# Turning the convolution branch, the heads' outputs and the memory's tokens with VectorE and transfers of GpSimd

## The chip, the cores and the metric

The kernel runs on one core of one Trainium2 chip. The core has five engines with instruction queues of their own: TensorE (PE, matrix products and transposes into PSUM), VectorE (DVE), ScalarE (ACT), GpSimd (POOL) and SyncE (SP, which here only issues transfers). Each queue runs in order; engines and transfers wait for one another through semaphores. The metric is the device time of one execution in microseconds (us), lower is better.

## The reference

One layer of a streaming encoder on 512 tokens x 1024 channels in float32, with 256 memory tokens. Cut to what the change touches:

```python
h = _rms_norm(x, norm_mix_pre)
(a_q, a_k, a_v, f_q, f_k, f_v, f_g, c_u, s_x, s_b, s_c) = jnp.split(h @ w_in, cuts, axis=-1)
# A: differential attention, 4 heads of 128 output channels, each normed per token over its channels
ya = _diff_attention(a_q, a_k, a_v, lam, t_pos)
ya = _rms_norm(ya, diff_norm) * (1.0 - lambda_init)
# B: forgetting attention, 8 heads of 64
yf = _forgetting_attention(f_q, f_k, f_v, log_f, t_pos)
# C: gated unit, causal depthwise convolution over 31 tokens, LayerNorm over 512 channels, swish
yc = _dwconv_causal(c_a * jax.nn.sigmoid(c_g), conv_dw) + conv_dw_b
yc = jax.nn.silu(_layer_norm(yc, conv_ln_g, conv_ln_b))
# D: short convolution;  then  sum over branches of sigmoid(gate) * (branch @ w_branch), @ w_out, norm, residual
# cross-attention: m = _rms_norm(mem, norm_mem); keys and values are m @ w_xkv
# gated MLP with a depthwise convolution over 3 tokens
```

The three places share one problem: a result lies with channels on the partitions and is to be normed over channels (so tokens must be on the partitions), or the reverse.

## The kernel before

Every float32 product is made of three passes: both operands are split into a high part (float32r) and the rest, and `mm3` issues high x high, high x low and low x high. ScalarE writes the high part of a weight block (L190), VectorE the rest (L191), ahead of TensorE. A block is [128 x 8 x 128] weights against 512 tokens: 24 matmuls of 512 columns. `run_blocks` takes the blocks in a fixed order (`mixer_jobs`): the convolution's inputs, the D branch, the gates of D, the values of A (`v_jobs`), queries and keys of the four A heads (`qk_jobs`) with the gates of C between them, the values of the forgetting branch (`vf_jobs`), its queries and keys for four pairs of heads with the gates of A between them, then the gates of the forgetting branch, the output projection, cross-attention and the MLP.

Everything else is a background task, a Python generator that the planner `Background` advances between blocks: the first two tasks of its queue, by a credit of 0.7 per microsecond of its own clock, each step giving its cost and the time that must pass before the next (`yield cost, wait`). `drain` runs a task out at once. Afterwards the framework orders the instructions of each engine; `issue_after` holds an instruction behind another one of the same engine.

The tasks that the change touches:

- `conv_norm_task` (L670): when the four convolutions have ended (their ends are in `conv_ends`), VectorE transposes the result in 32x32 blocks (L676), SP writes it to DRAM with 128-byte runs in four transfers (L680) and reads it back with tokens on the partitions in four more (L683); VectorE norms it (L693 to L696), and the same way leads back to channels (`conv_chan`). ScalarE then makes two passes for each of four tiles (L705, L706), which are split into y["c"].
- `a_task` (L822): six steps of scores, softmax and values of one A head, then the tail: ScalarE copies the output from PSUM (L858), TensorE transposes it in four pieces (L863), ScalarE squares (L864), VectorE sums (L866) and scales it (L868), TensorE transposes back (L874), and `split` with the scale `half["dn"]` writes y["a"] (L877).
- `mem_task` (L1169): for each of two tiles of 128 memory tokens, load, norm (`normed`), and `to_channels` (L286), which transposes in eight pieces on TensorE and splits into `ns.mt`.
- `f_task` (L965): loads two rows of cumulative sums (`ck`, L972), then per step GpSimd makes a bias (`fbias`, L1002, L1004), TensorE the scores, and VectorE adds the two and takes the maximum (L1008).

TensorE's own transposes all go through `transpose` (L236). The tags `ck` and `fbias` have two buffers of [128 x 512] each, as have PSUM's `mm`, `av`, `sc` and `tr`.

Of the kernel before, what the change touches and what calls it, by code (L numbers as in the profile page):

```python
# [25 lines left out]
P = 128  # L26
# [57 lines left out]
def hybrid_layer(ctx: ExitStack, tc: tile.TileContext, a: dict, out: bass.AP):  # L84
# [584 lines left out]

    def conv_norm_task():  # L670
        xn = m1p.tile([P, 5, S], F32, tag="qk", name="xn", bufs=2)
        tok, chan = (dram.tile([S, S], F32, name=n) for n in ("conv_tok", "conv_chan"))

        def turn(rows, squares, src):
            for i in range(4):
                V.transpose(squares[:, i], src[:, i])  # L676
                yield 0.65, 0.0
            form = rows.rearrange("(b r) (j a c) -> a r j b c", r=32, a=4, c=32)
            for a in range(4):
                SP.dma_start(form[a], squares[a * 32:a * 32 + 32].rearrange("r j (b c) -> r j b c", c=32))  # L680
            yield 0.0, 4.0
            for i in range(4):
                SP.dma_start(xn[:, i], rows[i * P:(i + 1) * P, :])  # L683
            yield 0.0, 5.0

# [3 lines left out]
        yield from turn(tok, conv_u, conv_y)  # L689
        for t in range(NT):  # L690
            st = m1p.tile([P, 6], F32, tag="bn6", name="bn6", bufs=2)
            mv = m1p.tile([P, 2], F32, tag="bn2", name="bn2", bufs=2)
            V.bn_stats(st, xn[:, t])  # L693
            V.bn_aggr(mv, st)
            r = rstd_of(m1p, [mv[:, 1:2]])
            V.tensor_scalar(xn[:, t], xn[:, t], mv[:, 0:1], r, ALU.subtract, ALU.mult)  # L696
            yield 1.5, 0.0
        yield from turn(chan, conv_y, xn)
# [4 lines left out]
        for j in range(4):  # L703
            e = e4()
            A.activation(e[:, 0], xn[:, j], AF.Identity, bias=pc("ln_b", j), scale=pc("ln_g", j))  # L705
            A.activation(e[:, 1], xn[:, j], AF.Tanh, bias=half["ln_b"][:, j:j + 1], scale=half["ln_g"][:, j:j + 1])  # L706
# [55 lines left out]

    def qk_jobs(cq, ck, j, then):
# [5 lines left out]
        def body_q(hi, lo):  # L769
# [5 lines left out]
            for c, r in enumerate(rows):  # L775
                A.copy(qk[r, c], ps[r])
                V.tensor_tensor(qk[rows[1 - c], c], ps[r], qk[r, c].bitcast(F32), ALU.subtract)  # L777
# [43 lines left out]

    def a_task(h, qk, v):  # L822
        es, pt, av = {}, None, None
        for step in range(6):
# [31 lines left out]
            if step == 5:  # L856
                e = e4()
                A.copy(e[:, 0], av)  # L858
            yield cost, 3.5

        ps = bank("tr")
        for t in range(NT):
            transpose(ps[:, t * P:(t + 1) * P], e[:, 0, t * P:(t + 1) * P])  # L863
        A.activation(e[:, 1], ps, AF.Square, scale=1.0 / math.sqrt(P))  # L864
        ms = m1p.tile([P, NT], F32, tag="ms4", name="ms4", bufs=2)
        V.tensor_reduce(ms, e[:, 1].rearrange("p (t c) -> p t c", t=NT), AX.X, ALU.add)  # L866
# [6 lines left out]
        for t in range(NT):  # L873
            transpose(ps2[:, t * P:(t + 1) * P], e[:, 0, t * P:(t + 1) * P])  # L874
# [880 lines left out]
```

## Time and profile before

| | |
|---|---|
| median of 3 runs | 1061.36 us (1061.24 to 1062.24) |
| profiled execution | 1061.46 us, span 1059.7 us |
| TensorE busy | 1048.7 us (99%) |
| VectorE, ScalarE, GpSimd busy | 800.8, 497.9, 150.8 us |
| transfers that GpSimd issues (queue q0) | 2560 packets, 8.54 MB |
| transfers that SP issues (queue q1) | 170659 packets, 124.10 MB |

In the profile's rows, "L232" is the line of the kernel, `out<-in` the tiles by the program's names, `128x512` partitions x elements. In an answer by line the three numbers are the shortest, middle and longest duration in ns, then the first and last start in us. In a timeline the first two columns are start and length in us, and brackets hold the idle time of the engine before the instruction and what ended it. In the list of waits come the waiting instruction, the one waited for, the total in us, the count and the longest.

### The profile page before, as it was taken

The page shows a single profiled execution, that of the slowest core. Times are in us where ns is not written, and L with a number is a line of the kernel's source. Part 1 is how long each engine was busy: PE and PEld are TensorE (multiplying, and loading weights), DVE is VectorE, ACT ScalarE, POOL GpSimd, SP SyncE. Part 2 cuts the span into 40 slices and gives each one's busy share as a digit, 9 for nine tenths or more (in the row PEclk, how much of TensorE's full clock was granted, in tenths as well). Part 3 has the DMA queues.
Part 4 walks back from the last instruction along what each step waited for, and adds up shares of the span by engine and source line. Part 5 has one row for each costly group of instructions (what it writes and reads, how often), then busy time and mean ns, then how long its engine had stood idle before and what let it go on. Part 6 is the DMA issues. An engine that isn't in the chain of part 4 may idle for free.

```text
span 1059.7 us, 14546 instructions
## 1 busy us (share of the span) xinstructions
PE 1048.7 (99%) x5343; PEld 891.8 (84%) x5343; DVE 800.8 (76%) x1270; ACT 497.9 (47%) x819; POOL 150.8 (14%) x249
## 2 busy tenths in 40 slices
PE   9999999999999999999999999999999999999997
PEld 8888888878888988888888899999888888888886
DVE  6999997577666358766575888886778788777796
ACT  5322222277465255655443665654333333445672
POOL 4001000100001015322100031031111211111011
PEclk9999999999999999999999999999999999999999
DMA  8854335732222243322344734226566776725662
GB/s 269 300 153 104 104 97 128 198 113 80 80 80 68 59 135 100 97 84 80 120 140 154 268 133 120 80 81 199 179 229 211 235 230 209 236 80 179 210 216 80
DMA packets 179773, 156.78 MB, mean 148 GB/s; under 512 B 22207, under 2 KB 151852, under 8 KB 179701
## 3 DMA queue, kind: packets, MB, share of 16 engines
q1 hardware_dynamic: 170659, 124.10, 38.9%
q10 hardware_dynamic: 6482, 23.21, 5.8%
q0 software_dynamic: 2560, 8.54, 2.8%
q8 instruction: 42, 0.69, 0.3%
q14 instruction: 30, 0.25, 0.1%
HBM read 135.89 MB, written 19.94 MB: 147 GB/s over the span
## 4 chain that ended last, share of the span: by engine, by line
PE 95%; DMA 1%; DVE 1%; ACT 1%; issue 0%; POOL 0%; SPq 0%; POOLq 0%; DVEq 0%; ACTq 0%
PE ps_mm L232 51%; PE ps_av L232 29%; PE ps_sc L232 7%; PE ps_tr L232 4%; PE ps_tr L236 3%; DMA xn<-conv_tok 1%; PE ps_mm L442 1%; PE ps_av L442 1%; DMA conv_chan<-y 0%; PE ps_mm L384 0%; SPq L680 0%; PE ps_sc L389 0%; DMA xn<-conv_chan 0%; DVE wl L191 0%; POOL st_r L271 0%
## 5 line engine op out<-in xcount | busy, mean ns | idle before, releaser
L190 ACT CAST wh<-wr 128x1024 fp32r<-128x1024 f32 (+1 forms) x142 | 148.6, 1049 | 273.5 <-PE ps_mm L232 185.6
L191 DVE TENSOR_TENSOR wl<-wr,wh 128x1024 fp32r<-128x1024 f32 (+1 forms) x142 | 178.1, 1256 | 80.9 <-ACT wh L190 80.3
L232 PE MATMUL ps_mm<-hth,wh 128*128 128x512 f32 (+1 forms) x616 | 231.4, 382 | 2.4 <-DVE qk L777 1.9
L232 PE MATMUL ps_mm<-htl,wh 128*128 128x512 f32 (+1 forms) x616 | 230.1, 380 | 0.0
L232 PE MATMUL ps_mm<-hth,wl 128*128 128x512 f32 (+1 forms) x616 | 229.9, 380 | 0.0
L232 PEld LDWEIGHTS ps_mm<-hth,wh 128*128 128x128 f32 x616 | 114.1, 188 | 24.5 <-issue 2.3
L232 PEld LDWEIGHTS ps_mm<-hth,wl 128*128 128x128 f32 x616 | 114.0, 188 | 21.3
L232 PEld LDWEIGHTS ps_mm<-htl,wh 128*128 128x128 f32 x616 | 114.1, 188 | 20.3
L232 PE MATMUL ps_av<-htl,wh 128*128 128x512 f32 (+1 forms) x328 | 122.5, 373 | 0.0
L232 PE MATMUL ps_av<-hth,wh 128*128 128x512 f32 (+1 forms) x328 | 122.4, 373 | 0.0
L232 PE MATMUL ps_av<-hth,wl 128*128 128x512 f32 (+1 forms) x328 | 122.4, 373 | 0.0
L664 DVE SCALAR_TENSOR_TENSOR y<-y,par,y 128x482 f32<-128x482 f32 (+29 forms) x120 | 82.9, 727 | 0.2
L232 PEld LDWEIGHTS ps_av<-hth,wh 128*128 128x128 f32 x328 | 61.6, 188 | 10.9
L232 PEld LDWEIGHTS ps_av<-hth,wl 128*128 128x128 f32 x328 | 61.6, 188 | 10.9
L232 PEld LDWEIGHTS ps_av<-htl,wh 128*128 128x128 f32 x328 | 61.6, 188 | 10.8
L1548 DVE TENSOR_TENSOR wl<-dw,wh 128x1024 fp32r<-128x1024 f32 x32 | 40.2, 1260 | 13.2 <-ACT wh L1547 13.0
L1547 ACT CAST wh<-dw 128x1024 fp32r<-128x1024 f32 x32 | 33.4, 1051 | 23.3 <-PE ps_tr L232 8.5
L1002 POOL TENSOR_SCALAR fbias<-ck,cq 128x128 f32<-128x128 f32 (+3 forms) x32 | 27.5, 865 | 68.9 <-DVE st L1008 63.7
L1496 ACT ACTIVATE th<-c 128x512 f32<-128x512 f32 x22 | 13.9, 632 | 48.3 <-DVE c L594 48.2
L155 ACT CAST pth<-ps_tr 128x512 fp32r<-128x512 f32 (+3 forms) x56 | 23.4, 448 | 22.0 <-PE ps_tr L236 21.9
L594 DVE SCALAR_TENSOR_TENSOR c<-ps_mm,par,c 128x510 f32<-128x510 f32 (+1 forms) x44 | 32.7, 744 | 0.7
L156 DVE TENSOR_TENSOR ptl<-ps_tr,pth 128x512 fp32r<-128x512 f32 (+3 forms) x56 | 27.9, 513 | 6.1 <-ACT pth L155 5.9
(469 smaller groups left out, 2102.9 us busy)
## 6 DMA issues: line engine op xcount, KB each, us to landing
wr<-in_w_up SPq DMA_DIRECT2D x44, 512.0 KB
wr<-in_w_in SPq DMA_DIRECT2D x38, 512.0 KB
wr<-in_w_gate SPq DMA_DIRECT2D x32, 512.0 KB
wp<-in_w_down ACTq DMA_DIRECT2D x22, 512.0 KB
sums<-wp ACTq DMA_DIRECT2D x22, 512.0 KB
dw<-sums SPq DMA_DIRECT2D x44, 256.0 KB
wr<-in_w_branch SPq DMA_DIRECT2D x16, 512.0 KB
wide<-in_w_out SPq DMA_DIRECT2D x12, 512.0 KB
```

The lines of the kernel that those rows point to most:

```text
L155: A.copy(hi, ps)
L156: V.tensor_tensor(lo, ps, hi.bitcast(F32), ALU.subtract)
L190: order(A.copy(hi, raw[:, :n]))
L191: low.tensor_tensor(lo, raw[:, :n], hi.bitcast(F32), ALU.subtract)
L232: PE.matmul(ps, lhs, rhs, start=start, stop=stop)
L236: PE.transpose(ps, x, ident[:n, :n])
L442: keep(PE.matmul(banks[c][:, :S // 2], w[p == 1][:, k, c * P:(c + 1) * P], ht[p == 2][:, i * 4 + k, :S // 2], start=(i, p, k) == (0, 0, 0) ...
L594: ins = V.scalar_tensor_tensor(dst[:, s:], src[:, :S - s], w(k), dst[:, s:], ALU.mult, ALU.add)
L664: ins = V.scalar_tensor_tensor(dst[:, s:], src[:, :S - s], pc("conv_dw", k * 4 + j), dst[:, s:], ALU.mult, ALU.add)
L1002: G.tensor_scalar(bias[:, :w], ck[j][:, :w], -1.0, cq[:, qt, head:head + 1], ALU.mult, ALU.add)
L1547: A.copy(hi, x)
L1548: V.tensor_tensor(lo, x, hi.bitcast(F32), ALU.subtract)
```

## The change

Three turns are made another way, and one start is held. A new helper `turn` transposes 32x32 blocks on VectorE (`squares` also groups the blocks), has GpSimd write the tile to DRAM in whole rows, and read it back in four transfers, one for each 32 partitions, whose runs are 128 x n / 4 floats long. The heads' tails use it twice in place of TensorE's transposes, in tiles of the tags `ck` and `fbias` instead of `e`; the back way adds one ScalarE pass (`Identity` with the scale) ahead of the split. The memory tiles use it once each, on the buffers that they already have. The convolution's turns keep their count of VectorE transposes, and their transfers become one write and four reads on GpSimd's queue. `f_task` for the first pair of heads makes no step until the second query block has been issued, and its first pass of VectorE stands behind that block's last eviction.

```diff
@@ -667,43 +667,71 @@
                 conv_ends.append(ins.ins)
             yield 0.66, 0.0
 
+    def squares(dst, src, n):
+
+        V.transpose(dst.rearrange("p (b n c) -> p n b c", b=4, c=32), src.rearrange("p (n b c) -> p n b c", b=4, c=32))
+
+    def turn(dst, src, n, between, name, blocks_first=False):
+
+        t = dram.tile([P, n * P], F32, name=name)
+        if blocks_first:
+            V.transpose(between, src)
+        else:
+            squares(between, src, n)
+        yield 0.1 + 0.14 * n, 0.5
+        G.dma_start(t, between)
+        yield 0.0, 4.0
+        form = t.rearrange("(i r) (b x) -> b r i x", r=32, b=4)
+        for b in range(4):
+            G.dma_start(dst[b * 32:b * 32 + 32].rearrange("r (i x) -> r i x", i=4), form[b])
+        yield 0.0, 5.0
+
     def conv_norm_task():
         xn = m1p.tile([P, 5, S], F32, tag="qk", name="xn", bufs=2)
-        tok, chan = (dram.tile([S, S], F32, name=n) for n in ("conv_tok", "conv_chan"))
-
-        def turn(rows, squares, src):
-            for i in range(4):
-                V.transpose(squares[:, i], src[:, i])
-                yield 0.65, 0.0
-            form = rows.rearrange("(b r) (j a c) -> a r j b c", r=32, a=4, c=32)
-            for a in range(4):
-                SP.dma_start(form[a], squares[a * 32:a * 32 + 32].rearrange("r j (b c) -> r j b c", c=32))
-            yield 0.0, 4.0
-            for i in range(4):
-                SP.dma_start(xn[:, i], rows[i * P:(i + 1) * P, :])
-            yield 0.0, 5.0
-
+        tok, chan = (dram.tile([P, NT * S], F32, name=n) for n in ("conv_tok", "conv_chan"))
         yield 0.0, 2.0
         while len(conv_ends) < 4:
             yield 0.0, 0.5
-        yield from turn(tok, conv_u, conv_y)
+
+        sq = conv_u.rearrange("p j c -> p (j c)").rearrange("p (b t j c) -> p j t b c", b=4, t=NT, j=4)
+        for j in range(4):
+            V.transpose(sq[:, j], conv_y[:, j].rearrange("p (t b c) -> p t b c", t=NT, b=4))
+            yield 0.65, 0.0
+        G.dma_start(tok, conv_u.rearrange("p j c -> p (j c)"))
+        yield 0.0, 4.0
+        form = tok.rearrange("(a r) (b x) -> b r a x", r=32, b=4)
+        for b in range(4):
+            G.dma_start(xn[b * 32:b * 32 + 32, :4], form[b])
+        yield 0.0, 5.0
+        tokens = xn[:, :4].rearrange("p a (t x) -> p t a x", t=NT)
+        sq = conv_y.rearrange("p j c -> p (j c)").rearrange("p (a j t c) -> p t a j c", a=4, j=4, t=NT)
         for t in range(NT):
             st = m1p.tile([P, 6], F32, tag="bn6", name="bn6", bufs=2)
             mv = m1p.tile([P, 2], F32, tag="bn2", name="bn2", bufs=2)
-            V.bn_stats(st, xn[:, t])
+            V.bn_stats(st, tokens[:, t])
             V.bn_aggr(mv, st)
             r = rstd_of(m1p, [mv[:, 1:2]])
-            V.tensor_scalar(xn[:, t], xn[:, t], mv[:, 0:1], r, ALU.subtract, ALU.mult)
+            V.tensor_scalar(tokens[:, t], tokens[:, t], mv[:, 0:1], r, ALU.subtract, ALU.mult)
             yield 1.5, 0.0
-        yield from turn(chan, conv_y, xn)
+        for t in range(NT):
+            V.transpose(sq[:, t], tokens[:, t].rearrange("p a (j c) -> p a j c", j=4))
+            yield 0.65, 0.0
+        G.dma_start(chan, conv_y.rearrange("p j c -> p (j c)"))
+        yield 0.0, 4.0
+        form = chan.rearrange("(b r) (a x) -> a r b x", r=32, a=4)
+        for a_ in range(4):
+            G.dma_start(xn[a_ * 32:a_ * 32 + 32, :4], form[a_])
+        yield 0.0, 5.0
+        turned_y = xn[:, :4].rearrange("p b (j t c) -> p j t b c", j=4, t=NT)
         while "d" in y:
             yield 0.0, 2.0
         yield 0.0, 2.0
         y["c"] = (y8(), y8())
         for j in range(4):
             e = e4()
-            A.activation(e[:, 0], xn[:, j], AF.Identity, bias=pc("ln_b", j), scale=pc("ln_g", j))
-            A.activation(e[:, 1], xn[:, j], AF.Tanh, bias=half["ln_b"][:, j:j + 1], scale=half["ln_g"][:, j:j + 1])
+            one, two = (e[:, i].rearrange("p (t b c) -> p t b c", t=NT, b=4) for i in range(2))
+            A.activation(one, turned_y[:, j], AF.Identity, bias=pc("ln_b", j), scale=pc("ln_g", j))
+            A.activation(two, turned_y[:, j], AF.Tanh, bias=half["ln_b"][:, j:j + 1], scale=half["ln_g"][:, j:j + 1])
             V.scalar_tensor_tensor(e[:, 0], e[:, 1], 1.0, e[:, 0], ALU.add, ALU.mult)
             split(e[:, 0], y["c"][0][:, j], y["c"][1][:, j], 0.5)
             yield 1.4, 1.0
@@ -760,6 +788,8 @@
 
             yield *cols(w_in, c0, BR, kb * 2, 2), body
 
+    query_ends = {}
+
     def qk_jobs(cq, ck, j, then):
 
 
@@ -774,7 +804,8 @@
             channel_major(ps, (hi, lo), ht)
             for c, r in enumerate(rows):
                 A.copy(qk[r, c], ps[r])
-                V.tensor_tensor(qk[rows[1 - c], c], ps[r], qk[r, c].bitcast(F32), ALU.subtract)
+                low = V.tensor_tensor(qk[rows[1 - c], c], ps[r], qk[r, c].bitcast(F32), ALU.subtract)
+            query_ends[cq, j] = low.ins
 
         def body_k(hi, lo):
             qk = st["qk"]
@@ -818,6 +849,9 @@
         return (m1p.tile([P, 4, 256], F32R, tag="pth", name="pth", bufs=2),
                 m1p.tile([P, 4, 256], F32R, tag="ptl", name="ptl", bufs=2))
 
+
+    def head_tile(tag):
+        return m1p.tile([P, S], F32, tag=tag, name=f"head_{tag}", bufs=2)
 
     def a_task(h, qk, v):
         es, pt, av = {}, None, None
@@ -854,27 +888,29 @@
                                        ALU.subtract)
                 cost += 0.6 + 0.0035 * w
             if step == 5:
-                e = e4()
-                A.copy(e[:, 0], av)
+                o = head_tile("ck")
+                A.copy(o, av)
             yield cost, 3.5
 
-        ps = bank("tr")
-        for t in range(NT):
-            transpose(ps[:, t * P:(t + 1) * P], e[:, 0, t * P:(t + 1) * P])
-        A.activation(e[:, 1], ps, AF.Square, scale=1.0 / math.sqrt(P))
+        sq = head_tile("fbias")
+        x = head_tile("ck")
+        yield from turn(x, o, NT, sq, f"head_tok{h}")
+        A.activation(sq, x, AF.Square, scale=1.0 / math.sqrt(P))
         ms = m1p.tile([P, NT], F32, tag="ms4", name="ms4", bufs=2)
-        V.tensor_reduce(ms, e[:, 1].rearrange("p (t c) -> p t c", t=NT), AX.X, ALU.add)
+        V.tensor_reduce(ms, sq.rearrange("p (a t c) -> p t a c", a=4, t=NT), AX.XY, ALU.add)
         r = rstd_of(m1p, [ms], NT)
-        V.tensor_tensor(e[:, 0].rearrange("p (t c) -> p t c", t=NT),
-                        ps.rearrange("p (t c) -> p t c", t=NT),
-                        r.unsqueeze(2).to_broadcast([P, NT, P]), ALU.mult)
-        yield 1.5, 3.5
-        ps2 = bank("tr")
-        for t in range(NT):
-            transpose(ps2[:, t * P:(t + 1) * P], e[:, 0, t * P:(t + 1) * P])
+        x4 = x.rearrange("p (a t c) -> p a t c", a=4, t=NT)
+        V.tensor_tensor(x4, x4, r.unsqueeze(1).unsqueeze(3).to_broadcast([P, 4, NT, 32]), ALU.mult)
+        yield 1.5, 1.0
+        o = head_tile("ck")
+        sq = head_tile("fbias")
+        yield from turn(o, x, NT, sq, f"head_chan{h}", True)
         if "a" not in y:
             y["a"] = (y8b(), y8b())
-        split(ps2, y["a"][0][:, h], y["a"][1][:, h], half["dn"])
+        z = head_tile("fbias")
+        A.activation(z.rearrange("p (t b c) -> p t b c", t=NT, b=4), o.rearrange("p (b t c) -> p t b c", b=4, t=NT),
+                     AF.Identity, scale=half["dn"])
+        split(z, y["a"][0][:, h], y["a"][1][:, h])
         yield 0.6, 0.0
 
 
@@ -972,6 +1008,8 @@
             G.dma_start(t, crows[2 * p + j:2 * p + j + 1, :].rearrange("a s -> (a s)").partition_broadcast(P))
             ck.append(t)
         yield 0.0, 2.0
+        while p == 0 and (O_FQ, 1) not in query_ends:
+            yield 0.0, 0.5
         es, pts, av = {}, None, None
         for step in range(6):
             if step in (3, 5):
@@ -1005,9 +1043,10 @@
                                     compare_op=ALU.is_ge, fill=BIG, base=0, channel_multiplier=1)
                     ps = bank("sc")
                     scores(ps, qk, j, qt * P, w)
-                    V.tensor_tensor_reduce(e[:, j, :w], ps[:, :w], bias[:, :w], scale=1.0,
-                                           scalar=-3.0e38, op0=ALU.add, op1=ALU.max,
-                                           accum_out=st[:, j:j + 1])
+                    with tc.issue_after(query_ends[O_FQ, 1]) if p + step == 0 else ExitStack():
+                        V.tensor_tensor_reduce(e[:, j, :w], ps[:, :w], bias[:, :w], scale=1.0,
+                                               scalar=-3.0e38, op0=ALU.add, op1=ALU.max,
+                                               accum_out=st[:, j:j + 1])
                 V.tensor_scalar(st[:, 2:4], st[:, 0:2], -HD ** -0.5, None, ALU.mult)
                 for j in range(2):
                     A.activation(e[:, j, :w], e[:, j, :w], AF.Exp, bias=st[:, 2 + j:3 + j],
@@ -1173,9 +1212,13 @@
             y_t = normed(ns.xm, m_t, [ns.gain], stage("s2", "mn"))
             if t == 0:
                 space(ns.xm, "gap8", 96)
-            yield 1.3, 8.0
-            to_channels(y_t, ns.mt, t)
-            yield 1.2, 0.0
+            yield 1.3, 3.0
+            yield from turn(y_t, y_t, NK, m_t, f"mem_chan{t}")
+            by_chan = y_t.rearrange("p (b k c) -> p k b c", b=4, k=NK)
+            for i in range(2):
+                ks = slice(i * 4, i * 4 + 4)
+                split(by_chan[:, ks], *(x[:, ks, t * P:(t + 1) * P].rearrange("p k (b c) -> p k b c", b=4) for x in ns.mt))
+                yield 0.7, 1.0
 
     def kx_jobs():
         for h in range(4):
```

## The prediction

> **What bounds the kernel now.** I read the page first, then the waits of TensorE, then stretches of the span, then single instructions. Page: the span, the busy times, and the chain of work that ended last.
>
> ```profile
> span 1059.7 us, 14546 instructions
> PE 1048.7 (99%) x5343; PEld 891.8 (84%) x5343; DVE 800.8 (76%) x1270; ACT 497.9 (47%) x819; POOL 150.8 (14%) x249
> PE 95%; DMA 1%; DVE 1%; ACT 1%; issue 0%; POOL 0%; SPq 0%; POOLq 0%; DVEq 0%; ACTq 0%
> ```
>
> TensorE is busy 99% of the span and is 95% of the chain. Because ends of matmuls are modelled, "busy" could hide gaps, so I look at who kept TensorE waiting (first the total, then the count, then the longest):
>
> ```profile
> PE ps_mm L232 <- DVE qk L777: 1.9, 1, 1.9
> PE ps_mm L384 <- DVE e L335: 1.3, 1, 1.3
> PE ps_mm L442 <- ACT hth L432: 0.2, 1, 0.2
> ...
> ```
>
> In the whole run there is one stall of TensorE in the middle, 1.9 us, and 1.3 us at the start; the rows behind are of 0.2 us. So instructions taken off TensorE shorten the run one for one, and work put on any other engine is free until TensorE waits for it. The stretches that the change touches (us, PE, PEld, DVE, ACT, POOL busy, clock, DMA share, GB/s):
>
> ```profile
> 224.00:270.00 46.00, 46.00 (x236) 39.03 (x235) 31.99 (x87) 31.55 (x72) 2.08 (x4) 1.00 0.27 81
> 270.00:340.00 70.00, 70.00 (x354) 59.09 (x354) 46.19 (x110) 38.26 (x79) 6.68 (x11) 1.00 0.25 76
> 510.00:580.00 70.00, 70.00 (x334) 58.54 (x333) 42.25 (x58) 27.91 (x41) 3.34 (x7) 1.00 0.40 125
> ```
>
> TensorE is full in all three. VectorE is at 60 to 70%, ScalarE at 40 to 69%, GpSimd below 10%, the DMA engines at 25 to 40%, and the clock is full. There is room for every kind of work that the change adds.
>
> **What comes off TensorE.** Each of four heads loses two groups of four transposes, and each of two memory tiles loses eight. The length that a row gives a group (0.60 us for four) includes latency; its price is the step from start to start:
>
> ```profile
> 276.55 0.39 PE L232 MATMUL ps_mm<-hth,wl 128*128 128x512 f32 x1
> 276.78 0.60 PE L236 MATMUL ps_tr<-ident,e 128*128 128x128 f32 x4
> 277.13 0.48 PE L232 MATMUL ps_mm<-hth,wh 128*128 128x512 f32 x1
> 277.45 0.40 PE L232 MATMUL ps_mm<-htl,wh 128*128 128x512 f32 x1
> ...
> 541.79 1.04 PE L236 MATMUL ps_tr<-ident,mn 128*128 128x128 f32 x8
> 542.59 0.48 PE L232 MATMUL ps_mm<-y,wl 128*128 128x512 f32 x1
> 542.90 0.63 PE L232 MATMUL ps_mm<-y,wh 128*128 128x512 f32 x2
> ```
>
> An ordinary 512-wide matmul steps 276.78 - 276.55 = 0.23 us. Four transposes take 0.35 us, and the matmul behind them steps 0.32 us, 0.09 more than usual: 0.44 us a group. Eight take 0.80 us and the matmul behind them 0.31: 0.88. Sum: 8 x 0.44 + 2 x 0.88 = 5.3 us off the path, certain, since the new code issues no transposes there and TensorE is the bound in each place.
>
> The page VectorE: DVE Perf Modes of the Trainium skill, under its rules for kernel authors, says to use TensorE for a 128x128 transpose if a PSUM destination will do, and the DMA crossbar otherwise. By that rule the sum would not gain the 5.3 us and the first rival below would be the likely one; the windows above speak against it here, since the 0.44 us belong to the one full engine.
>
> **What is added for the heads**, with rows for its parts: VectorE's transpose, the head's copy, square, sum, scaling, GpSimd's issue of a 256 KB transfer and its landing.
>
> ```profile
> L676 DVE STREAM_TRANSPOSE y<-xn x4: 671/680/705, 195.1 to 199.2; 128x512 f32<-128x512 f32 x4
> L858 ACT COPY e<-ps_av x4: 575/586/589, 264.9 to 349.8; 128x512 f32<-128x512 f32 x4
> L864 ACT ACTIVATE e<-ps_tr x4: 598/599/604, 270.0 to 353.2; 128x512 f32<-128x512 f32 x4
> L158 ACT ACTIVATE y8b<-ps_tr,s_dn x4: 672/688/690, 279.7 to 359.8; 128x512 fp32r<-128x512 f32 x4
> ...
> L972 POOL DMA_DIRECT2D ck<-crows x8: 536/578/698, 389.0 to 464.9; - x8
> DMA to landing us min/median/max: 3.5/4.0/4.5
> ...
> 408.56 0.62 PE L232 MATMUL ps_mm<-y8b,wh 128*128 128x512 f32 x2
> ```
>
> Per head: two VectorE transposes (1.4 us), one more ScalarE pass (0.6), ten GpSimd issues (5.8). None lies on TensorE. One turn lasts 0.68 + a write (4.0) + three issues before the last read (1.7) + its landing (4.0) = 10.4 us; two turns with about 5 us of norm and split between and after make 26 us from the copy. The last head is copied at 349.8, so it would be ready at 376. Its first reader runs at 408.56: 32 us of cover. Without that cover every us would stall gate blocks of the first branch.
>
> Queues. On GpSimd's queue the four reads wait for the write, and behind them stand the zeroing of query tiles and the small powers of the norms; on ScalarE the square and the last scaling wait for a landing, with casts of weights and of queries and keys behind them. What such a wait can do is seen once in this run, in the convolution's turn (ScalarE, then TensorE); the last row is ScalarE's waits for weights:
>
> ```profile
> 211.09 0.81 ACT L705 ACTIVATE e<-xn,par 128x512 f32<-128x512 f32 x1 [2.04 <-DMA xn<-conv_chan]
> ...
> 220.76 0.39 PE L232 MATMUL ps_mm<-hth,wl 128*128 128x512 f32 x1
> 223.02 0.47 PE L232 MATMUL ps_mm<-hth,wh 128*128 128x512 f32 x1 [1.87 <-DVE qk L777]
> ...
> ACT wh L190 <- DMA wr<-in_w_in: 13.5, 6, 4.9
> ```
>
> ScalarE stood 2.04 us for the landing, its eight convolution passes then ran late into the eviction of a query block, and TensorE lost 223.02 - 220.76 - 0.23 = 2.03 us. But there a burst of some 8 us stood behind the wait. A head has one or two passes of 0.6 us there, and a bank of TensorE is refilled for 24 x 0.23 = 5.5 us while the other is evicted, so a wait of 2 us is mostly covered. Bounds for the eight waits of the heads: nothing, and 8 x 2.03 = 16.2 us. I take 1.0 us, near the lower end: ScalarE also waited six times for weights, up to 4.9 us, and no stall of TensorE answers to them.
>
> **The convolution.** The count of VectorE's transposes stays; SP's sixteen transfers become ten of GpSimd.
>
> ```profile
> 199.87 5.41 SPq L680 DMA_DIRECT2D conv_chan<-y  x4
> 205.38 1.26 SPq L176 DMA_DIRECT2D wr<-in_w_in  x1
> 208.52 1.77 SPq L683 DMA_DIRECT2D xn<-conv_chan  x4
> ...
> L1241 POOL DMA_DIRECT2D xin<-in_x x4: 527/552/589, 580.1 to 630.7; - x4
> DMA to landing us min/median/max: 3.7/6.1/9.6
> ```
>
> SP spent 5.41 us issuing the four scattered writes, with a weight load held up behind them; that goes. From the last transpose to the first scaling pass it took 211.09 - 199.87 = 11.2 us. The new way: one write of 1 MB, for which the nearest rows are the 512 KB loads that GpSimd issues (last two lines: 3.7 to 9.6 us to the landing, median 6.1), so I estimate 6 to 8 us; four reads of 256 KB, 1.7 + 4.0 us. That is 11.7 to 13.7: 0.5 to 2.5 us later than now, and now every pass needs all four reads. On the other side GpSimd's transfers don't stand behind weight loads in SP's queue, and the order of ScalarE is drawn anew around them. The 2.03 us stall can go (-2.0) or grow by the 2.5 us. I take 0.
>
> **The memory tiles** add one 128x1024 VectorE transpose and five GpSimd transfers each, one tile after the other since both use the same two buffers.
>
> ```profile
> L1172 POOL DMA_DIRECT2D m_t<-in_mem x2: 541/568/594, 505.5 to 537.8; - x2
> ...
> 617.96 0.28 PE L232 MATMUL ps_av<-mth,wh 128*128 128x256 f32 x1
> ```
>
> The first tile's load is issued at 505.5, the second's at 537.8 now; each tile then takes some 15 us for its turn, so the second ends near 580 at the latest, and its first reader is at 617.96. Cost 0, with over 30 us of cover; behind them on GpSimd's queue stand only gain and residual loads for the same late stage.
>
> **The held scores.** The first forgetting head's steps begin after the second query block is evicted, and its first pass on VectorE stands behind that eviction.
>
> ```profile
> L1008 DVE CUSTOM_DVE_ANT_0 e<-ps_sc,fbias x32: 273/482/693, 393.4 to 507.1; 128x128 f32<-128x128 f32 x8, 128x256 f32<-128x256 f32 x8, 128x384 f32<-128x384 f32 x8, 128x512 f32<-128x512 f32 x8
> ...
> DVE e L1008 <- POOL fbias L1004: 3.2, 2, 2.4
> ...
> L776 ACT CAST qk<-ps_mm x16: 571/582/586, 218.8 to 477.9; 64x512 fp32r<-64x512 f32 x16
> ```
>
> Now the first pass is at 393.4, and VectorE waited up to 2.4 us for GpSimd's bias. Held back, it starts some 3 us later, and the query eviction no longer stands behind that wait. The end of this stage is set by the fourth pair of heads: the last query block is evicted at 477.9 and its keys come one block of 5.5 us later, 90 us behind the first pair, so the 3 us don't reach the end. Cost 0; if that cover were gone, 3 us.
>
> **Sum.** Against the profiled execution (1061.46 us, 1059.7 of span): -5.3 + 1.0 + 0 + 0 + 0 = -4.3, so 1057.2; the median of the runs is 0.1 lower, which I leave out. The three runs lie within 1.0 us, so 0.2% (2.1 us) is about what can be told from no change: faster means below 1059.2, slower above 1063.5.
>
> **Rivals.**
>
> Late landings reach TensorE (0.14). ScalarE's and VectorE's waits on the heads' transfers are passed on as in the convolution's turn: 1061.5 - 5.3 + 16.2 = 1072.4 if all eight are, 1064.3 if half are. It decides from 7.4 / 2.03, four such stalls, on. For: that stall. Against: the cover of 5.5 us per bank, and ScalarE's idle 31 to 60%.
>
> The planner starts the later heads too late (0.14). It works on two background tasks at a time. A head's tail used to carry 3.5 + 3.5 us of its clock as waits; now it carries 3.5 + 9.5 + 1 + 9.5 = 23.5, so heads three and four start up to 16 us later, and part of their attention is left to be drained as the value projection of the forgetting branch begins, which wants both banks that the head's output occupies. Then TensorE idles for the last head's chain: passes of 0.7 us on VectorE and ScalarE, some 9 us from scores to copy, less the products that don't need that bank. I price it at 2 to 5 us: 1058 to 1061, around the border of no change.
>
> GpSimd's issues are starved (0.08). While VectorE is at work, a GpSimd operation can take far longer than its own time:
>
> ```profile
> L1002 POOL TENSOR_SCALAR fbias<-ck,cq x32: 371/588/2065, 392.7 to 502.7; 128x128 f32<-128x128 f32 x8, 128x256 f32<-128x256 f32 x8, 128x384 f32<-128x384 f32 x8, 128x512 f32<-128x512 f32 x8
> ```
>
> The spread 371 to 2065 ns is partly size; the excess over the median is 1.5 us. If each of the sixteen turns' stages of the heads were late by that, and half of it stalled TensorE: 16 x 1.5 / 2 = 12 us, 1068. Against it: GpSimd's issues of transfers in the same stretch took 536 to 698 ns. The page SBUF — State Buffer of the Trainium skill, under Summary: rules for kernel authors, says that GpSimd's making of descriptors is starved while VectorE runs in its fast two-port modes, and to issue from SP or ScalarE what is to hide under VectorE's work; the issue times of this run don't show it.
>
> That the change does not do what it says can be left out: the transposes are gone from the code.
>
> **How the numbers follow.** Forecast 0.64, its own range 1054 to 1059.2: the low end is the forecast less the 2.0 us of the convolution's stall and the 1.0 us that I charged. The rivals hold 0.14, 0.14 and 0.08. Faster is the forecast's case, 0.64; no change the planner's, 0.14; slower the other two, 0.22. The range runs from 1053.5 to 1065.5, over half of the late-landing case; above it lie about 0.1.
>
> **What would show it.** The groups of transposes of the memory tiles vanish from TensorE, and those of the heads' outputs with them (48 instructions). TensorE's waits stay under 4 us in total, with none over 2.5. The last head's split ends before 390, the second memory tile's before 590, ScalarE's waits on the heads' landings are below 3 us each. Wrong it would be if TensorE's waits rise to 8 us or more between 200 and 400 us, with rows that name a query or key eviction (late landings) or the output copy of a head (the planner), or if GpSimd's issues take over 1 us.

## The result and the profile after

The changed kernel takes 1065.52 us (median of 5 runs, 1064.21 to 1067.40); the kernel before, beside it, 1061.24. The ratio is 1.004, 95% interval 1.0021 to 1.0059: slower by some 4 us, where 1057.2 was predicted. The profiled execution took 1065.52 us with a span of 1063.4, 3.7 more than before.

The page of the changed kernel (span, busy times, chain):

```profile
span 1063.4 us, 14555 instructions
PE 1044.1 (98%) x5295; PEld 886.6 (83%) x5295; DVE 806.0 (76%) x1280; ACT 501.1 (47%) x823; POOL 183.2 (17%) x309
PE 88%; DVE 4%; DMA 3%; issue 2%; ACT 2%; POOL 1%; POOLq 0%; DVEq 0%; ACTq 0%
```

The 48 transposes are gone (TensorE's instructions fall from x5343 to x5295) and TensorE is busy 4.6 us less. But it is no longer 95% of the chain: 88%. Its waits, changed kernel (us in total, count, longest):

```profile
PE ps_mm L232 <- DVE qk L807: 2.7, 1, 2.7
PE ps_mm L232 <- DVE v L156: 1.6, 1, 1.6
PE ps_mm L384 <- DVE e L335: 1.3, 1, 1.3
PE ps_mm L232 <- DVE htl L156: 0.7, 1, 0.7
PE ps_av L232 <- ACT head_ck L892: 0.7, 1, 0.7
PE ps_av L232 <- ACT pth L155: 0.7, 1, 0.7
PE ps_mm L232 <- DVE htl L1591: 0.4, 1, 0.4
PE ps_av L232 <- DVE ptl L156: 0.3, 1, 0.3
PE ps_mm L442 <- ACT hth L432: 0.2, 1, 0.2
PE ps_mm L232 <- ACT hth L155: 0.2, 1, 0.2
```

They sum to 8.8 us; before it was 3.8 (five rows: 1.9, 1.3 and three of 0.2). So 4.6 us less work and 5.0 us more waiting: TensorE's last matmul ends 0.3 us later than before, and the whole gain is gone. Of the 5.0, 3.1 lie around the last head's output and the values behind it, 0.8 in the convolution's stall, and 1.1 in two single waits for VectorE's splits (`htl`, near 643 and 1038 us) whose cause no run here shows. The other loss lies behind TensorE, in the closing of the program, which the engines' busy times don't count. There each engine's queue runs DRAIN instructions. The instructions of the line that opens and closes the program (L1751 before, L1794 after; duration ns min/median/max, then first and last start in us), kernel before:

```profile
L1751 POOLq DRAIN  x3: 40/93/2799, 1054.7 to 1059.4; - x3
L1751 SPq DRAIN  x3: 7/7/7, 1058.9 to 1059.2; - x3
```

and the changed kernel:

```profile
L1794 POOLq DRAIN  x3: 46/98/7707, 1054.9 to 1063.1; - x3
L1794 SPq DRAIN  x3: 7/7/7, 1059.1 to 1062.9; - x3
```

GpSimd's first closing DRAIN begins 0.2 us later than before and lasts 7.71 us instead of 2.80. Before, it was over at 1057.5, ahead of SP, whose last output transfer was done at 1058.9. After, SP is done at 1059.1 and all engines wait for GpSimd until 1062.6. That is 1062.6 - 1059.1 = 3.5 us; with the 0.2 us it makes the 3.7.

Where TensorE waits anew: its instructions around the last head's output, changed kernel (start us, us, instruction, idle before it and who ended that):

```profile
351.87 0.60 PE L236 MATMUL ps_tr<-ident,e 128*128 128x128 f32 x4
353.15 0.38 PE L232 MATMUL ps_av<-pth,v 128*128 128x256 f32 x1 [0.67 <-ACT pth L155]
353.87 0.38 PE L232 MATMUL ps_av<-ptl,v 128*128 128x256 f32 x1 [0.34 <-DVE ptl L156]
...
356.04 0.39 PE L232 MATMUL ps_av<-wh,hth 128*128 128x264 f32 x1 [0.68 <-ACT head_ck L892]
...
372.32 0.50 PE L232 MATMUL ps_mm<-hth,wh 128*128 128x512 f32 x1 [1.60 <-DVE v L156]
```

The last head's probabilities are transposed, split and multiplied with nothing between, and the forgetting values (`wh,hth`, 264 wide) wait for the copy that empties the `av` bank. The fourth wait comes through ScalarE: its cast of a weight block waited 3.0 us for the load, and the casts of the values stood behind it.

```profile
369.62 1.05 ACT L190 CAST wh<-wr 128x1024 fp32r<-128x1024 f32 x1 [3.01 <-DMA wr<-in_w_in]
```

The copies of the heads' outputs (the prediction shows the row of before, last start 349.8) now end later:

```profile
L892 ACT COPY head_ck<-ps_av x4: 586/588/588, 265.5 to 355.4; 128x512 f32<-128x512 f32 x4
```

The same stretch by windows, first the kernel before, then the changed one (window, length, PE, PEld, DVE, ACT, POOL busy, clock, DMA share, GB/s):

```profile
340.00:380.00 40.00, 40.00 (x280) 37.47 (x280) 18.66 (x37) 15.10 (x24) 1.21 (x2) 1.00 0.29 80
```

```profile
340.00:380.00 40.00, 36.71 (x262) 34.20 (x261) 22.61 (x51) 17.73 (x31) 14.53 (x26) 1.00 0.38 111
```

TensorE lost 3.3 us there. The other stall that grew is the convolution's (2.7 us, 1.9 before). ScalarE's first convolution pass, in the changed kernel, starts 2.0 us later than before (211.09), though it waited less for its landing (2.04 before):

```profile
213.06 0.81 ACT L733 ACTIVATE e<-xn,par 128x512 f32<-128x512 f32 x1 [1.43 <-DMA xn<-conv_chan]
```

and the landings of GpSimd's eight reads into `xn`, from the issue, in the same run:

```profile
DMA to landing us min/median/max: 4.3/5.3/6.2
```

### The profile page after: what moved, and what is told of

The parts are those of the page before. It is cut to its first block, busy times and chain, and to the rows that moved or that the text cites. A ratio compares the mean times of both kernels' runs of the same rounds, so it can differ in the third digit from the quotient of the medians.

```text
span 1063.4 us, 14555 instructions
## 1 busy us (share of the span) xinstructions
PE 1044.1 (98%) x5295; PEld 886.6 (83%) x5295; DVE 806.0 (76%) x1280; ACT 501.1 (47%) x823; POOL 183.2 (17%) x309
## 3 DMA queue, kind: packets, MB, share of 16 engines
q0 software_dynamic: 5824, 19.03, 5.9%
## 4 chain that ended last, share of the span: by engine, by line
PE 88%; DVE 4%; DMA 3%; issue 2%; ACT 2%; POOL 1%; POOLq 0%; DVEq 0%; ACTq 0%
PE ps_mm L232 48%; PE ps_av L232 27%; PE ps_sc L232 6%; PE ps_tr L232 3%; PE ps_tr L236 2%; DMA dw<-sums 1%; DVE wl L191 1%; DMA xn<-conv_chan 1%; DMA xn<-conv_tok 1%; PE ps_mm L442 1%; DVE wl L1591 1%; PE ps_av L442 1%; PE ps_mm L384 0%; ACT wh L190 0%; DMA wr<-in_w_in 0%
```

## The experiments

Theory: three things take back the 5.3 us and some 4 us more. GpSimd's closing DRAIN grows with the number of transfers that GpSimd issued (3.5 us); the longer tails of the heads fill the two places of the planner, so that the last head's attention is given out together with the forgetting values (some 4 us); the convolution's reads land late at times (1 to 5 us). Rivals: the DRAIN goes by bytes or packets; the heads' transfers themselves cause the stalls; the memory tiles or the held scores have a share. Three groups of runs were made, each with its own runs of the kernel before beside it; a ratio is against these.

**Sixty more transfers of GpSimd, in the kernel before** (e1_sixty_rows)

```diff
+                    for _ in range(1 + n % 2):
+                        r = next(rows)
+                        G.dma_start(extra[r:r + 1], ident[0:1])
```

> The kernel before with 60 more transfers that GpSimd issues in the up projection (one row of 512 bytes each, SBUF to a scratch tensor; they feed nothing). Count theory: GpSimd's closing DRAIN lasted 2.80 us before and 7.71 us after, and GpSimd issued 26 transfers before and 86 after, so 4.91 / 60 = 0.082 us for each; here 86 again, a DRAIN of 7.7 us, and the end 3.4 us later than before (the DRAIN has about 1.5 us of cover behind the last output transfer), 1064.8. Packet theory: it goes by what is moved (3264 more packets, 10.5 MB); 60 packets of 512 bytes add below 0.1 us, DRAIN 2.8 to 2.9, time as before, 1061.4. In both TensorE's waits stay at the 4 us of before, within 0.5.

```profile
L1756 POOLq DRAIN  x3: 40/93/7703, 1080.9 to 1089.1; - x3
...
L1516 POOL DMA_DIRECT2D extra<-ident x60: 484/484/824, 2.4 to 43.3; - x60
```

The DRAIN takes 7.70 us, as in the changed kernel, with sixty transfers of 512 bytes: the count decides, not what is moved (GpSimd's queue q0 moved 4480 packets and 8.58 MB here, 5824 packets and 19.03 MB in the changed kernel). The time, 1092.47 us (ratio 1.0287, 1.0271 to 1.0303), was missed widely for another reason: the extra transfers depend on nothing, so they were put at the very start of GpSimd's queue (second row), among the small operations of the first norms, and TensorE waited:

```profile
25.40 1.12 PE L426 MATMUL ps_tr<-ident,nt 128*128 128x128 f32 x4 [17.17 <-DVE nt L421]
```

That accident says one thing more: the sixty had landed at most 5.7 us after their issue, and the DRAIN paid for them a thousand us later. It does not wait for transfers in flight.

**The turns' transfers on SP** (e2_turns_on_sp)

```diff
-        G.dma_start(t, between)
+        SP.dma_start(t, between)
...
-            G.dma_start(dst[b * 32:b * 32 + 32].rearrange("r (i x) -> r i x", i=4), form[b])
+            SP.dma_start(dst[b * 32:b * 32 + 32].rearrange("r (i x) -> r i x", i=4), form[b])
```

> The changed kernel with all 60 transfers of the turns issued by SP instead of GpSimd. Count theory: 26 transfers of GpSimd are left, DRAIN 2.8 us, the end 3.4 us nearer to the last matmul: about 1062.1 if TensorE's new stalls (5.4 us more than before) stay where they are, as the planner theory says, since the order of emission is the same. Rival, SP's queue: the turns' transfers stand behind weight loads that wait for a buffer, and weight loads behind them; ScalarE's waits for landings then exceed 3 us, TensorE's stalls grow by over 3 us more, and the gain of 3.4 us is lost: 1065 or more.

1073.23 us (ratio 1.0107, 1.0090 to 1.0123). The DRAIN is 2.80 us again with 26 transfers, but the rival's queue is real. TensorE and ScalarE waits of this kernel:

```profile
PE ps_mm L232 <- DVE v L156: 9.4, 2, 7.8
...
ACT wh L190 <- DMA wr<-in_w_in: 21.8, 7, 5.5
ACT wh L155 <- DMA wide<-out_sums: 9.1, 2, 7.5
```

ScalarE waited 5.5 us for a weight load issued behind the convolution's write, then 4.7 us for the convolution's reads; six convolution passes stood ahead of its casts of the values, and TensorE stood 7.8 us. The last row belongs to the output projection, where TensorE lost another 2.2 us. GpSimd's queue was the better one for the turns; only its DRAIN had no price in the prediction.

**The heads alone** (e3_heads_only): before, with the changed `a_task`, `turn` and `squares`

```diff
+        yield from turn(x, o, NT, sq, f"head_tok{h}")
...
+        yield from turn(o, x, NT, sq, f"head_chan{h}", True)
```

> The kernel before with the heads' part alone (turns by VectorE, GpSimd issues 40 more transfers; convolution, memory tiles and forgetting scores as before). Planner theory: transposes 8 x 0.44 = 3.5 us off TensorE, but the heads' last steps are crowded ahead of the forgetting values as in the changed kernel, +4.5 us of stalls between 340 and 380; DRAIN 2.8 + 40 x 0.082 = 6.1 us, of which some 1.8 us lie behind the output: 1061.4 - 3.5 + 4.5 + 1.8 = 1064.2. Rival, the stalls of 340 to 380 come from another part of the change (its convolution's lateness, or the held scores): no new stall there, 1059.7.

1065.86 us (ratio 1.0037, 1.0025 to 1.0049), 1.7 above what was expected, on the theory's side: the stalls around the last head are there without the rest of the change. The window of this kernel, and its row for the values:

```profile
340.00:380.00 40.00, 36.58 (x255) 34.35 (x254) 21.14 (x46) 16.30 (x30) 13.18 (x24) 0.96 0.36 102
```

```profile
PE ps_mm L232 <- DVE v L156: 1.7, 1, 1.7
```

The stalls are those of the changed kernel, but here the granted clock of TensorE is 0.96 in the window, where the changed kernel's was 1.00. It fell to 0.66 between 355 and 360 us, and to 0.81 and 0.85 in the two stretches of 5 us from 220 on, behind the convolution's stall of 1.9 us, which the kernel before has too, at 1.00. Matmuls of 512 columns stepped 0.43 us there instead of 0.23. So a stall can cost more than its length: TensorE is busy 1048.8 us here and 1045.5 in e8 below, with the same 5311 instructions, 3.3 us. That is in the profiled execution (1066.88 us); the runs spread from 1063.49 to 1067.68. The DRAIN with 66 transfers is

```profile
L1778 POOLq DRAIN  x3: 46/98/6065, 1058.3 to 1064.8; - x3
```

**Tails as tasks of their own** (e4_own_tails)

```diff
             yield cost, 3.5
+        bg.add(a_tail(h, o), "t")
 
+    def a_tail(h, o):
         sq = head_tile("fbias")
...
+        yield then(lambda: bg.drain("t"))
         ga = gate_blocks(0, "a")
```

> The changed kernel with each head's turns put into a background task of their own, which is not drained ahead of the forgetting values but one query and key pair later; the attention steps no longer queue behind the turns' waits in the planner. Planner theory: TensorE's excess over its ideal steps between 340 and 380 us falls from 5.1 to below 1.5 us, DRAIN stays 7.7 us: 1065.5 - 4 = 1061.5. Rival, the turns themselves (their transfers beside the weight loads, ScalarE's waits) make the stalls: they move with the tails, to 360 to 400 us, and 4 us or more of TensorE's stalls are left there: 1065.

1068.72 us (ratio 1.0060, 1.0039 to 1.0082): a miss. The four waits were all there, a few us later; TensorE's waits of this kernel:

```profile
PE ps_mm L232 <- DVE qk L807: 7.4, 1, 7.4
PE ps_mm L232 <- DVE v L156: 1.7, 1, 1.7
...
PE ps_av L232 <- ACT head_ck L892: 0.7, 1, 0.7
PE ps_av L232 <- ACT pth L155: 0.7, 1, 0.7
PE ps_av L232 <- DVE ptl L156: 0.3, 1, 0.3
```

That is not the rival either, since the stalls belong to the same products, not to the tails. The edit missed its aim: a tail task stands in the same queue and takes one of the same two places, so by the planner's rule, as its code reads, the last head's last steps were still left to the drain; its output was copied only at 361.4. The first row is the convolution's stall, at 7.4 us, with the convolution's code untouched. Its reads' landings in this run:

```profile
DMA to landing us min/median/max: 4.7/6.0/9.7
```

and ScalarE's wait for them, 6.1 us where the changed kernel had 1.4:

```profile
217.20 0.81 ACT L733 ACTIVATE e<-xn,par 128x512 f32<-128x512 f32 x1 [6.09 <-DMA xn<-conv_chan]
```

**Short planner waits in the heads' turns** (e5_short_waits)

```diff
-        yield 0.0, 4.0
+        yield 0.0, 4.0 * pause
...
-        yield 0.0, 5.0
+        yield 0.0, 5.0 * pause
...
-        yield from turn(x, o, NT, sq, f"head_tok{h}")
+        yield from turn(x, o, NT, sq, f"head_tok{h}", pause=0.0)
```

> The changed kernel with the two planner waits of a head's turn (4.0 and 5.0 of its clock) set to 0, so that a head's tail leaves the planner's two places sooner and the last head's attention steps are given out before the forgetting values, not with them (separating the tails did not do that: they kept one of the two places). Planner theory: TensorE's stalls at 352 to 371 us go, the excess over ideal steps between 340 and 380 us falls from 5.1 to 1.5 us or less, DRAIN stays 7.7: 1065.5 - 4 = 1061.5. Rival, the order of the planner isn't the cause but the transfers' landings: the stalls stay 4 us or more, 1065 or above, since work that waits for a landing now stands earlier in the queues.

1061.56 us (ratio 1.0012, 0.9998 to 1.0025), as the planner theory said: the same transfers, the same DRAIN (7.70 us), and the median is 0.6 us above its runs of before where the changed kernel's was 4.3, so 3.7 us less. (Three of the eleven runs took 1065.3 to 1066.9; why isn't shown.) The window of this kernel:

```profile
340.00:380.00 40.00, 40.00 (x275) 37.13 (x274) 21.19 (x41) 15.60 (x27) 8.91 (x16) 1.00 0.40 112
```

and its copies of the outputs:

```profile
L892 ACT COPY head_ck<-ps_av x4: 563/586/587, 266.3 to 348.2; 128x512 f32<-128x512 f32 x4
```

TensorE is full, the last copy is at 348.2 instead of 355.4, and all four waits of the changed kernel around it are gone. The two numbers changed are no waits of the chip: they only tell the planner when to give out the next piece.

**The memory tiles alone** (e6_memory_only)

```diff
-            yield 1.3, 8.0
-            to_channels(y_t, ns.mt, t)
+            yield 1.3, 3.0
+            yield from turn(y_t, y_t, NK, m_t, f"mem_chan{t}")
```

> The kernel before with the memory tiles' part alone (their turns by VectorE, ten more transfers of GpSimd). Theory: 16 transposes off TensorE, 2 x 0.88 = 1.8 us; DRAIN 0.68 + 36 x 0.0817 = 3.6 us, which ends before the last output transfer does, so it costs nothing: 1061.4 - 1.8 = 1059.6. Rival, the memory part also carries the stall of 0.9 us near 642 us of the changed kernel: 1060.5.

1059.06 us (ratio 0.9979, 0.9970 to 0.9988): 1.9 us faster than its runs of before (1061.0), for 1.8 expected. The DRAIN, 3.62 us with 36 transfers, is hidden, and neither of the two `htl` waits is there.

**The convolution alone** (e7_conv_only): before, with the changed `conv_norm_task`

```diff
-                SP.dma_start(form[a], squares[a * 32:a * 32 + 32].rearrange("r j (b c) -> r j b c", c=32))
+        G.dma_start(chan, conv_y.rearrange("p j c -> p (j c)"))
```

> The kernel before with the convolution's part alone (ten transfers of GpSimd in place of SP's sixteen). No transposes come off TensorE; DRAIN 3.6 us, hidden. Theory: the reads land 4.7 to 9.7 us after their issue beside a weight load, and what the last of them is late goes through ScalarE to TensorE's stall at 220 us, 2.9 us in one run of the changed kernel and 7.5 us in one with the same convolution, against 2.0 before: runs between 1061 and 1067, median 1 to 3 us above before, 1063.5. Rival, the convolution's part is neutral (the 7.5 us came from another order on an engine): 1061.4, with the narrow spread of before.

1063.45 us (ratio 1.0023, 1.0009 to 1.0036), between 1060.46 and 1067.95: 2.4 us slower in the median and spread over 7.5 us, where before spread over 4.0. In its profiled execution (1066.21 us, 2.8 above the median) the landings and TensorE's longest wait were

```profile
DMA to landing us min/median/max: 4.3/5.3/8.7
```

```profile
PE ps_mm L232 <- DVE qk L807: 5.7, 1, 5.7
```

**The heads with fewer old transfers** (e8_heads_fewer): e5's waits, convolution and memory as before

```diff
-            G.dma_start(t, crows[2 * p + j:2 * p + j + 1, :].rearrange("a s -> (a s)").partition_broadcast(P))
+            SP.dma_start(t, crows[2 * p + j:2 * p + j + 1, :].rearrange("a s -> (a s)").partition_broadcast(P))
...
-        G.dma_start(ns.gain, a["norm_mem"][0].partition_broadcast(P))
+        SP.dma_start(ns.gain, a["norm_mem"][0].partition_broadcast(P))
```

> The changed kernel with the heads' part and the held scores alone, short planner waits as in e5, and 20 of the 26 transfers that GpSimd issued before (gains, vectors of lambda, cumulative rows and their broadcasts) issued by SP; convolution and memory tiles as before. GpSimd issues 46: DRAIN 0.68 + 46 x 0.0817 = 4.4 us, level with the end of the last output transfer. Theory: 8 x 0.44 = 3.5 us off TensorE, no crowding, DRAIN nearly hidden: 1061.4 - 3.5 + 0.2 = 1058.1. Rival, SP's queue: the moved transfers stand between weight loads, TensorE's stalls grow by 3 us or more: 1061 or above.

1058.43 us (ratio 0.9971, 0.9961 to 0.9981), 0.3 from the expected time; DRAIN 4.43 us. The heads' part is a gain once its two side costs are gone: TensorE is busy 3.2 us less than before, for 3.5 expected. No run has the moved transfers alone, so what they add isn't shown.

**Heads and memory tiles together** (e9_heads_mem_fewer, and e10_heads_mem_fewest with the last six old transfers on SP; the lines are what e10 has beyond e9)

```diff
-            G.dma_start(m_t, mem_d[t * P:(t + 1) * P, :])
+            SP.dma_start(m_t, mem_d[t * P:(t + 1) * P, :])
...
-            G.dma_start(ns.x[t], x_d[t * P:(t + 1) * P, :])
+            SP.dma_start(ns.x[t], x_d[t * P:(t + 1) * P, :])
```

> As e8 (heads' part, held scores, short planner waits, 20 old transfers moved from GpSimd to SP) with the memory tiles' part added; the convolution as before. GpSimd issues 56: DRAIN 0.68 + 56 x 0.0817 = 5.3 us, of which 0.9 us lie behind the end of the last output transfer. The parts add up: e8's 1058.4 - 1.8 (memory tiles' transposes) + 0.9 = 1057.5. Rival, the two parts get in each other's way (the memory tiles' loads and gains now on SP): 1059 or above.

> As e9 with the last six old transfers (four loads of x, two of mem) moved to SP too. GpSimd issues 50: DRAIN 4.8 us, 0.4 us behind the output: 0.5 us less than e9, 1057.0. Rival, SP's weight loads stand behind these six and TensorE waits: 1058 or above.

1058.30 us (0.9969, 0.9958 to 0.9981) and 1057.47 us (0.9963, 0.9949 to 0.9976), 0.8 and 0.5 above what was expected. The second has the lowest median, below both kernels. That it lies near the 1057.2 of the prediction doesn't bear that out: it is another kernel, with the convolution as before, without the long planner waits and with fewer transfers of GpSimd. The intervals of e8, e9 and e10 overlap: which of the three is fastest isn't shown. The closing DRAIN of e10, with 50 transfers:

```profile
L1785 POOLq DRAIN  x3: 40/102/4768, 1049.8 to 1055.1; - x3
```

**Without the held scores** (e11_no_hold)

```diff
-        while p == 0 and (O_FQ, 1) not in query_ends:
-            yield 0.0, 0.5
```

> The changed kernel without the held scores (no wait in the planner, no order behind the second query block's eviction). The prediction had the hold at 0 us: 1065.5, within 1. Rival, the hold is part of the loss: TensorE's excess between 380 and 420 us falls and the time with it by over 2 us, 1063.

1064.68 us (ratio 1.0035, 1.0020 to 1.0050): no difference from the changed kernel (1.0040) that these runs can tell.

**A copy beside the convolution's reads** (e12_conv_copy_beside)

```diff
+        beside = dram.tile([P, NT * S], F32, name="beside")
+        G.dma_start(beside, chan)
         form = chan.rearrange("(b r) (a x) -> a r b x", r=32, a=4)
```

> The kernel before with the convolution's part alone (as e7) and one more 1 MB transfer, DRAM to DRAM, that GpSimd issues just ahead of the four last reads. In four traces the latest of these reads landed 6.1, 6.2, 8.7 and 9.7 us after its issue and TensorE's stall at 220 us was 2.4, 2.9, 5.8 and 7.5 us. Contention theory: what moves beside the reads sets when they land, so the extra 1 MB makes the latest landing 10 to 14 us, the stall 7 to 11 us (about the landing less 2 to 3), the median 1067 to 1071. Rival, the lateness is drawn by something else (the making of GpSimd's descriptors, say): landing 5 to 9.7 us as before, median about 1063.5.

1068.66 us (ratio 1.0070, 1.0053 to 1.0087): 7.2 us above its runs of before, where e7 was 2.4 above its own. Landings and TensorE's waits:

```profile
DMA to landing us min/median/max: 4.2/6.2/10.0
```

```profile
PE ps_sc L232 <- ACT qk L818: 6.1, 1, 6.1
PE ps_sc L232 <- DVE qk L819: 1.2, 1, 1.2
```

The median fits contention. The landing, 10.0 us, is at the low end of what was expected and hardly above the 9.7 us of e4, and the order of the engines was drawn anew by the edit: the stall is now at another product (`ps_sc`). Part of the time is the lower clock behind the stall: TensorE is busy 1051.1 us here and 1049.5 in e7, with the same 5343 instructions. So it is shown that a copy of 1 MB ahead of the reads costs time, but not through which of these, and not that such traffic is what varies from run to run in the kernels without the copy. That stays open, and so does the rival, a late making of the descriptors.

## Why the prediction was wrong

**What comes off TensorE** was right. 5.3 us were worked out from two groups; TensorE is busy 4.6 us less, the memory tiles alone gain 1.9 for 1.76, and the heads alone, with their side costs taken away, 1061.0 - 1058.4 = 2.6 for 3.5. That a us off TensorE is a us off the run held in e6, where no stall and no visible closing was added.

**The step that failed first is the sum: it had no term for the end of the run.** The prediction counted GpSimd's ten issues per head (5.8 us) and wrote that none lies on TensorE. True, but the end of the run is not TensorE's: behind it comes the closing, where GpSimd pays again for each transfer that it issued. The missing term was 3.5 us. The trace of before held a hint, a closing DRAIN of 2.80 us on a queue that had nothing left to do; one number, with no second one to tell what it grows with.

**The second is the planner, left out of the sum as a rival.** That rival had the right place, the right bank and the right price (2 to 5 us; 3.1 us by the waits, 3.7 by e5). Its chance, 0.14, was the error: 3.5 + 3.5 against 23.5 us of the planner's waits stood in the text, and that sum decides which steps are left to the drain. It could have been followed through the code before the run, and then belongs into the sum, not among the rivals. With the sizes measured since, the sum would have been 1061.46 - 5.3 + 1.0 + 3.7 + 3.5 = 1064.4.

**The convolution** was taken at 0 with bounds of -2.0 and +2.5. In the profiled execution of the changed kernel the stall grew by 0.8 us only; the part alone costs 2.4 us in the median of e7, at the upper bound, and single runs go beyond it (7.4 us of stall in e4 against 1.9). The estimate treated a landing as one number; it is a spread (4.2 to 10.0 us over these runs), and what is behind it in ScalarE's queue passes on the late end. Nor did it have a price for the lower clock that can follow a stall.

**The heads' waits**, charged at 1.0 us: ScalarE waited for their landings twice in the changed kernel, and no wait of TensorE answers to it.

```profile
ACT head_fbias L898 <- DMA head_ck<-head_tok: 0.7, 1, 0.7
ACT head_fbias L911 <- DMA head_ck<-head_chan: 0.6, 1, 0.6
```

The cover worked, and the first rival, late landings, did not come from the heads. Three more rows of the changed kernel: the last head's split, the memory tiles' splits, and a group of GpSimd's issues (busy us, mean ns of one):

```profile
383.27 0.69 DVE L156 TENSOR_TENSOR y8b<-head_fbias,y8b 128x512 fp32r<-128x512 f32 x1 [0.71 <-ACT y8b L155]
```

```profile
L155 ACT CAST mth<-mn x4: 607/616/622, 553.7 to 573.6; 128x512 fp32r<-128x512 f32 x4
```

```profile
L686 POOL DMA_DIRECT2D head_ck<-head_tok x16 | 8.7, 553 | 6.5 <-DMA head_tok<-head_fbias 4.7 <-ACT v L155 1.8
```

The head is ready before 390, the second memory tile before 590, both as told; **the memory tiles** at 0 hold. **The held scores** at 0: e11 agrees. **Starved issues**: 553 ns each, and the heads' reads landed 2.1 to 4.6 us after their issue (median 2.2), no sign of it. So the warning on the page SBUF — State Buffer of the Trainium skill (Summary: rules for kernel authors) is not borne out by the heads' transfers in this trace, which doesn't show whether VectorE ran in the modes that the page names; the page's advice to issue from SP cost some 7.5 us more in e2, through SP's queue.

**The rule on transposes** of the Trainium skill (VectorE: DVE Perf Modes, rules for kernel authors) would keep them on TensorE. Here e6 and e10 are faster without them, by 1.9 and 4.0 us (1061.42 - 1057.47, with GpSimd's older transfers moved to SP too): the measurement differs from the rule where TensorE is the one full engine.

**What would show it**: TensorE's waits sum to 8.8 us instead of under 4, one above 2.5, and the rows named are the output copy of a head and a query eviction, the two given as signs of error. Between 200 and 400 us they come to 6.0, below the 8 that were given as the sign. No sign had been named for the end of the run.

## What to carry to other kernels

Look at what closes the program as well as at what fills it: an engine that is idle at the end can still hold the end, and its closing may grow with what it issued long ago. Where code with costs and waits of its own decides the order of work, new waits there are a cost to be followed through to the next drain, as closely as an instruction. A transfer that lands in front of a burst of work is to be priced by the late end of its landings, and a stall by the slower stretch that can follow it as well as by its length.

## What the runs showed of the hardware

GpSimd's closing DRAIN goes by the number of transfers that it issued: 2.80 us for 26, 3.62 for 36, 4.43 for 46, 4.77 for 50, 5.25 for 56, 6.07 for 66 and 7.70 to 7.71 for 86, of which sixty were once 64 KB to 1 MB and once 512 bytes. From the first and the last that is 4.91 / 60 = 0.082 us for each and 0.67 us beside; the others lie within 0.02 us of it, and so does e12 (37 transfers, 3.70). In this kernel it is covered up to some 4.3 us, an estimate from the starts of the closing DRAINs of GpSimd and SP, so by (4.3 - 0.67) / 0.082 = 44 transfers. Why it does so, the runs don't show.

Behind a stall of TensorE the granted clock can be lower for some us: 0.81 and 0.85 behind 1.9 us in e3, 0.50 behind 7.8 us in e2, but 1.00 behind the same 1.9 us in the kernel before and 2.7 us in the changed one. By TensorE's busy time for the same instructions that cost 3.3 us in e3 (against e8) and 4.8 us in e2 (1048.9 against the changed kernel's 1044.1). What decides whether it happens, the runs don't show.
